# A two-layer gMLP and dilated-attention trunk in fp32: where the terms of a seven-product matrix multiplication are formed, on which engine, and when the first stage's side loads are issued

## Chip, cores and metric

The kernel runs on one core of a Trainium2 chip. TensorE (PE) multiplies 128x128 weight tiles with blocks of up to 512 columns and sums in PSUM banks; VectorE (DVE), ScalarE (ACT) and GpSimd (POOL) work on tiles of 128 partitions; SyncE (SP) and ACT issue the DMAs that bring data in and out. Each engine works through its own queue in order and waits on semaphores of the others. The metric is the device time of one launch in microseconds (us).

## What is computed

The input x is 1024 positions by 1024 channels, in float32. Two layers follow each other, each with a token mixer and a squared-ReLU MLP, all with RMS norms ahead and residual sums behind. The MLP and the skeleton, with the MLP width 4096:

```python
def reference(x, mix_norm_g, mlp_norm_g, final_norm_g, a_w_in, a_ln_g, a_ln_b, a_w_s, a_b_s,
              a_w_out, b_w_qkv, b_w_out, rel_bias, w_up, w_down):
    h = x
    for layer in range(DEPTH):
        y = _rms_norm(h, mix_norm_g[layer])
        j = layer // N_MIXERS
        if layer % N_MIXERS == 0:
            y = _chunk_gating_mixer(y, a_w_in[j], a_ln_g[j], a_ln_b[j], a_w_s[j], a_b_s[j], a_w_out[j])
        else:
            y = _dilated_attention_mixer(y, b_w_qkv[j], b_w_out[j], rel_bias)
        h = h + y
        y = _rms_norm(h, mlp_norm_g[layer])
        h = h + jnp.square(jax.nn.relu(y @ w_up[layer])) @ w_down[layer]
    return _rms_norm(h, final_norm_g)
```

The gating mixer of layer 0 makes u and v (1024 columns each) by a GELU of a matrix product, normalizes v, mixes it over the 128 positions of a chunk with a causal 128x128 matrix for each of 8 channel groups (`a_w_s`, with the bias `a_b_s`), multiplies by u, and projects. The attention of layer 1 has three groups of 8 heads of width 64 with windows and dilations (128, 1), (512, 4), (2048, 16), and 4608 columns of q, k and v.

## The kernel before

**Tiles.** The residual h lies in SBUF as eight blocks `h[k]` of 128 channels by 1024 positions; most work is done in halves of 512 positions, s = 0 and 1. A float32 matrix is used as a high part (`hi`, rounded to the matmul format, written by ACT at L203 or with a scale at L517) and a low part (`lo`, the remainder, written by VectorE at L204 or L518); a product is three matmuls, hi.hi, lo.hi, hi.lo (L180). So each operand tile costs one ACT and one VectorE instruction ahead of TensorE. Weights arrive by SP's queue in a ring of four buffers `r` (L169).

**The start.** `w_v`, the half of the first weights that makes v, is used in three passes `gi` over chunks of 128 positions (three, three and two); in each pass k runs over the eight channel blocks, with 18 matmuls per k in the first two passes. In pass 0 `load_x(0, k)` (L508) brings the block of the first half, and `scaled(0, k)` makes its two parts, the tiles called y (L517, L518), and the squares for the norm (L252 on ACT, L261 on GpSimd). From k = 4 on, pass 0 also loads two blocks of the second half for each k; in pass 1 `scaled(1, k)` makes their parts, right where TensorE uses them. `gate_weights`, added at k = 1 of pass 0, loads the causal matrices and their bias on ACT's queue (L532, L537), masks them on GpSimd (L533), splits them (`wsh`, `wsl`, L203) and forms `rb` from a matmul with ones. `spatial`, added at the start of pass 1, normalizes v chunk by chunk and does the chunk mixing with `wsh`, `wsl` and `rb`.

**Seven products.** The wide products (MLP up, q/k/v) use a scheme with seven products of half blocks in place of eight. `Terms` holds the seven x operands: t[1], t[2], t[3] are plain blocks of the normalized input (`keep` for the first half of the positions, `raws` for the second), and t[4] to t[7] are differences of them: with y0, y1 the two channel halves of `keep` and z0, z1 those of `raws`, they are z0 - y0, z1 - t1, z1 - z0 and (z1 - z0) - t2 in the code's names. `first` and `second` are generators that make the blocks and differences (L469 the block, L476 and L477 two differences on VectorE, L478 and L479 two on GpSimd); `rest` splits two of the four terms of each block later (with a copy on GpSimd, L490). This is done three times: for the MLP of layer 0, for the attention and for the MLP of layer 1. While the terms aren't ready, the first two pairs of output tiles are made the plain way (`classical`), four PSUM banks for each half; in `mlp` these are evicted by `squared` (Relu at L688, Square at L689), in the attention by `out` (L1079 for v tiles, L1121 on ACT and L1122 on VectorE for the two parts of q and k). Then `mlp` goes on with the products for q = 2: the first product's bank is copied by `first_sum` (L750) so that it can be used again.

**Order.** TensorE's order is that of the code, with a `Flow`: generators added by `flow.add` yield a modelled time or an event, and `flow.pump()`, called between groups of matmuls, lets those go on whose time has come by the model. ACT, VectorE, GpSimd and SP are ordered by a scheduler; `tc.high_priority(offset=PRIO)` moves an instruction ahead there. In the attention, `attention()` is such a generator: the scores of a unit are matmuls of k and q (at L180, with 64 partitions).

## Time and profile before

| | us |
|---|---|
| median of 3 runs | 2182.33 |
| lowest, highest | 2180.11, 2182.43 |
| the profiled execution | 2182.13 |
| its span in the trace | 2180.4 |

The profile is of one execution. Its span begins with the first and ends with the last instruction; the other 1.7 us lie around it. TensorE is busy in nearly all of it. In a timeline row stand the start, the length, engine, line, operation, the names of the tiles written and read, the shape and the count of merged instructions; in brackets the idle time ahead and what ended it. A row of windows has the busy time and count of each engine in a stretch, the clock that TensorE was granted as a share of full speed, and the share of the DMA engines' time.

### The profile page before, as it was taken

How to read it: one execution, taken by the hardware profiler on the slowest of the kernel's cores; microseconds unless marked ns; L12 is line 12 of the kernel's file. 1: busy time of each engine (PE TensorE's matmuls, PEld its weight loads, DVE VectorE, ACT ScalarE, POOL GpSimd, SP SyncE). 2: the span in 40 equal slices, each digit the busy share in tenths (PEclk: the TensorE clock that was granted, in tenths of full speed). 3: DMA queues.
4: the chain of work that ended last, by engine and by line, in shares of the span. 5: the costliest groups of instructions: out<-in, count | busy, mean ns of one | idle time of the engine just before them, and what ended most of it. 6: DMA issues, size and time to landing. Idle time of an engine off the chain costs nothing.

```text
span 2180.4 us, 30158 instructions
## 1 busy us (share of the span) xinstructions
PE 2121.8 (97%) x10242; PEld 1755.2 (80%) x10242; DVE 1647.1 (76%) x2987; ACT 1126.3 (52%) x2266; POOL 600.9 (28%) x442
## 2 busy tenths in 40 slices
PE   7999999999999999998999999999999999999998
PEld 5888887888878888886888788887878888788887
DVE  5875349676689888878787877878786666988886
ACT  5743225555564444346665656665455555544443
POOL 1100115333223322533212222201343232333345
PEclk9999999999999999999999999999999999999999
DMA  6221213456354444321211111141055543644432
GB/s 222 87 88 45 62 41 96 158 189 198 138 176 160 159 141 137 105 82 39 52 46 46 43 48 45 46 147 62 20 169 193 184 159 113 203 150 146 157 104 78
DMA packets 158814, 247.04 MB, mean 113 GB/s; under 512 B 33481, under 2 KB 47940, under 8 KB 158660
## 3 DMA queue, kind: packets, MB, share of 16 engines
q1 hardware_dynamic: 157760, 243.89, 34.3%
q8 instruction: 80, 1.31, 0.2%
q10 hardware_dynamic: 900, 1.23, 0.2%
q14 instruction: 74, 0.61, 0.1%
HBM read 180.41 MB, written 64.66 MB: 112 GB/s over the span
## 4 chain that ended last, share of the span: by engine, by line
PE 82%; DVE 9%; ACT 3%; issue 2%; DMA 2%; POOL 0%; SPq 0%; DVEq 0%; ACTq 0%; POOLq 0%
PE at L180 41%; PE mm L180 39%; PE at L187 2%; DVE wp L204 2%; DVE t L204 1%; ACT t L1219 1%; ACT wp L203 1%; DVE k L1122 1%; DMA t<-hid 1%; DVE tr L204 0%; DMA r<-in_w_v 0%; DVE h L332 0%; DVE q L1122 0%; DVE h L893 0%; DMA h<-hd 0%
## 5 line engine op out<-in xcount | busy, mean ns | idle before, releaser
L203 ACT ACTIVATE wp<-r 128x512 fp32r<-128x512 f32 (+3 forms) x492 | 295.1, 605 | 458.0 <-PE at L180 287.7
L180 PE MATMUL mm<-y,wp 128*128 128x512 f32 x1608 | 405.2, 398 | 12.8 <-ACT t L750 6.6
L180 PE MATMUL at<-hx,wp 128*128 128x512 f32 x1770 | 413.8, 390 | 3.8 <-DVE wp L204 2.2
L204 DVE TENSOR_TENSOR wp<-r,wp 128x512 fp32r<-128x512 f32 (+3 forms) x492 | 380.9, 778 | 40.1 <-ACT wp L203 36.3
L180 PEld LDWEIGHTS at<-hx,wp 128*128 128x128 f32 x1770 | 331.8, 188 | 75.1 <-DVE h L893 3.3
L180 PEld LDWEIGHTS mm<-y,wp 128*128 128x128 f32 x1608 | 303.2, 191 | 80.4 <-ACT t L750 7.5
L180 PE MATMUL at<-t,wp 128*128 128x512 f32 x1344 | 314.3, 389 | 0.0
L180 PEld LDWEIGHTS at<-t,wp 128*128 128x128 f32 x1344 | 252.7, 188 | 52.7 <-DVE t L756 0.2
L401 POOL TENSOR_TENSOR t<-r 128x512 f32<-128x512 f32 (+3 forms) x78 | 112.8, 1446 | 624.8 <-DMA r<-in_w_dn 270.3
L403 POOL TENSOR_TENSOR r<-r 128x512 f32<-128x512 f32 (+3 forms) x78 | 118.4, 1518 | 326.9 <-DVE wp L204 320.1
L180 PE MATMUL mm<-t,wp 128*128 128x512 f32 x768 | 192.6, 398 | 0.0
L204 DVE TENSOR_TENSOR hx<-t,hx 128x512 fp32r<-128x512 f32 x192 | 179.8, 948 | 5.7 <-ACT hx L203 5.6
L261 POOL TENSOR_TENSOR t<-t 128x512 f32<-128x512 f32 (+1 forms) x54 | 69.1, 1280 | 387.3 <-ACT t L252 385.4
L180 PE MATMUL mm<-hx,wp 128*128 128x512 f32 x708 | 171.8, 389 | 0.0
L180 PEld LDWEIGHTS mm<-t,wp 128*128 128x128 f32 x768 | 141.2, 189 | 29.8
L180 PE MATMUL mm<-y,whi 128*128 128x512 f32 x512 | 158.1, 390 | 0.0
L180 PEld LDWEIGHTS mm<-hx,wp 128*128 128x128 f32 x708 | 132.8, 188 | 28.1 <-DVE b L919 0.6
L893 DVE TENSOR_TENSOR h<-h,at 128x512 f32<-128x512 f32 x144 | 97.5, 679 | 55.4 <-PE at L180 55.3
L180 PE MATMUL at<-y,wp 128*128 128x512 f32 x552 | 138.1, 391 | 0.0
L756 DVE TENSOR_TENSOR t<-t,at 128x512 f32<-128x512 f32 x116 | 79.0, 683 | 74.9 <-PE at L180 74.7
L203 ACT ACTIVATE hx<-t 128x512 fp32r<-128x512 f32 x192 | 118.4, 628 | 27.8 <-DMA t<-hid 23.4
L406 POOL TENSOR_TENSOR r<-r 128x512 f32<-128x512 f32 (+3 forms) x78 | 107.2, 1374 | 79.8 <-issue 54.0
(213 smaller groups left out, 3244.0 us busy)
## 6 DMA issues: line engine op xcount, KB each, us to landing
t<-hid SPq DMA_DIRECT2D x194, 256.0 KB, 5.0
hid<-t SPq DMA_DIRECT2D x140, 256.0 KB, 2.7
r<-in_w_up SPq DMA_DIRECT2D x128, 256.0 KB, 2.8
r<-in_w_dn SPq DMA_DIRECT2D x88, 256.0 KB, 2.7
r<-in_w_qkv SPq DMA_DIRECT2D x72, 256.0 KB, 2.6
hid<-b SPq DMA_DIRECT2D x56, 256.0 KB, 2.7
r<-in_w_v SPq DMA_DIRECT2D x48, 256.0 KB, 3.0
h<-in_xT SPq DMA_DIRECT2D x16, 256.0 KB, 4.5
```

The source lines that it names most:

```text
L180: nc.tensor.matmul(out, lhsT, rhs, **kw)
L187: nc.tensor.transpose(out, src, ident)
L203: nc.scalar.activation(hi, src, AF.Copy)
L204: nc.vector.tensor_tensor(lo, src, hi.bitcast(F32), op=ALU.subtract)
L261: nc.gpsimd.tensor_tensor(self.acc, self.acc, sq, op=ALU.add)
L401: tt(r3, r[0, 0], r[1, 0], op=ALU.subtract)
L403: tt(r[1, 1], r[1, 0], r[0, 0], op=ALU.subtract)
L406: tt(r[0, 0], r[0, 1], r[1, 1], op=ALU.subtract)
L756: nc.vector.tensor_tensor(out, x, y, op=ALU.add)
L893: engine.tensor_tensor(hs[i, s], hs[i, s], src, op=ALU.add)
L1122: nc.vector.scalar_tensor_tensor(lo, a, sc, hi.bitcast(F32), op0=ALU.mult, op1=ALU.subtract)
L1219: nc.scalar.activation(p[:, c], p[:, c], AF.Exp, bias=m, scale=-1.0, accum_out=dn)
```

## The change

- The gate's weights: `gate_weights` is added at k = 7 of pass 0 and issues its four loads and two masks first, then the splits; `rb` is formed with high priority, and an event `rb_done` is set behind it, which `spatial` waits for. The loads of the second half of x begin at k = 6 of pass 0, one for each k, and go on in pass 1; `scaled(1, k)` is called one k earlier.
- The terms: `second` forms all four differences of a block on VectorE, in place (only the one that is t[6] needs a further tile), and splits t[6] and t[7]; `rest` splits t[5] and t[4], after the flow has been moved on until `second` is done (`formed`). GpSimd has no part in it.
- The MLP's first pairs: the four Relus are issued first with high priority, the four Squares behind them without.
- The spill of h to memory (`hd`) ahead of the attention is issued in `second` rather than after `rest`, and the four evictions of the attention's second half are written in another order.

```diff
--- before.py
+++ after.py
@@ -442,7 +442,7 @@
         def __init__(self):
             self.blocks = {(j, s): [] for j in range(2) for s in range(2)}
             self.t = {1: self.blocks[0, 0], 2: self.blocks[1, 0], 3: self.blocks[1, 1], 4: [], 5: [], 6: [], 7: []}
-            self.kept = []
+            self.kept, self.formed = [], False
 
         def first(self, sq, gi):
 
@@ -458,7 +458,7 @@
                 yield LAT["tile"]
                 self.blocks[k // 4, 0].append(x)
 
-        def second(self, sq, gi):
+        def second(self, sq, gi, then=None):
             r = sq.rms()
             yield 2 * LAT["rms"]
             pb = spread(r)
@@ -470,29 +470,36 @@
                     x = pair().split(y)
                     yield LAT["tile"]
                     self.blocks[j, 1].append(x)
-            tt = nc.vector.tensor_tensor
-            for k, two in enumerate(raws):
-                (z0, z1), (y0, y1), t1, t2 = *([t[:, j, :] for j in range(2)] for t in (two, self.kept[k])), spare(), spare()
-                tt(t1, z0, y0, op=ALU.subtract)
-                tt(t2, z1, t1, op=ALU.subtract)
-                nc.gpsimd.tensor_tensor(y0, z1, z0, op=ALU.subtract)
-                nc.gpsimd.tensor_tensor(y1, y1, t2, op=ALU.subtract)
-                yield 2 * LAT["tile"]
-                self.t[5].append(pair("t1").split(t1))
-                self.t[6].append(pair("t2").split(t2))
+            if then:
+                then()
+            tt, sums = nc.vector.tensor_tensor, []
+            for k in range(5):
+                if k < 4:
+                    z, y, t = raws[k], self.kept[k], temp()
+                    tt(y[:, 0, :], z[:, 0, :], y[:, 0, :], op=ALU.subtract)
+                    tt(t, z[:, 1, :], y[:, 0, :], op=ALU.subtract)
+                    tt(y[:, 1, :], y[:, 1, :], t, op=ALU.subtract)
+                    sums.append(t)
+                if k:
+                    self.t[6].append(pair("t6").split(sums[k - 1]))
+                yield LAT["tile"]
+            for k in range(5):
+                if k < 4:
+                    tt(raws[k][:, 0, :], raws[k][:, 1, :], raws[k][:, 0, :], op=ALU.subtract)
+                if k:
+                    self.t[7].append(pair("t7").split(raws[k - 1][:, 0, :]))
+                yield LAT["tile"]
+            self.formed = True
 
         def rest(self):
 
-            for k, x in enumerate(self.kept):
-                t3, t4 = x[:, 0, :], x[:, 1, :]
-                if k == 3:
-                    t4 = temp()
-                    nc.gpsimd.tensor_copy(t4, x[:, 1, :])
-                self.t[7].append(pair("t3").split(t3))
-                self.t[4].append(pair("t4").split(t4))
-
-    def start_terms(sq, s, gi, terms):
-        flow.add((terms.second if s else terms.first)(sq, gi), (1 + s) * LAT["sum"])
+            flow.until(lambda: self.formed)
+            for i, p in ((0, 5), (1, 4)):
+                for x in self.kept:
+                    self.t[p].append(pair(f"t{p}").split(x[:, i, :]))
+
+    def start_terms(sq, s, gi, terms, *then):
+        flow.add((terms.second if s else terms.first)(sq, gi, *then), (1 + s) * LAT["sum"])
 
 
     vg = {}
@@ -526,23 +533,30 @@
 
     def gate_weights():
 
+        parts = []
         for i in range(2):
             wsr = temp()
             w3 = wsr.rearrange("p (g t) -> p g t", g=4)
             nc.scalar.dma_start(w3, w_s[:, 4 * i:4 * i + 4, :])
+            bs = temp()
+            nc.scalar.dma_start(bs, b_s[:, i * HALF:(i + 1) * HALF].partition_broadcast(P))
             nc.gpsimd.affine_select(w3, w3, pattern=[[0, 4], [1, P]], compare_op=ALU.is_ge, fill=0.0,
                                     base=0, channel_multiplier=-1)
-            split(wsh[:, 4 * i:4 * i + 4, :], wsl[:, 4 * i:4 * i + 4, :], w3)
-            bs = temp()
-            nc.scalar.dma_start(bs, b_s[:, i * HALF:(i + 1) * HALF].partition_broadcast(P))
-            yield 6000
+            parts.append((wsr, bs))
+        yield 5000
+        for i, (wsr, bs) in enumerate(parts):
+            split(wsh[:, 4 * i:4 * i + 4, :], wsl[:, 4 * i:4 * i + 4, :], wsr.rearrange("p (g t) -> p g t", g=4))
             ps = at_bank()
             matmul(ps, ones, wsr, passes=4, start=True, stop=True)
-            for g in range(4):
-                m = 4 * i + g
-                nc.vector.scalar_tensor_tensor(rb[:, m, :], ps[:, blk(g)], vec[:, 6, m:m + 1],
-                                               bs[:, blk(g)], op0=ALU.mult, op1=ALU.add)
-
+            with tc.high_priority(offset=PRIO):
+                for g in range(4):
+                    m = 4 * i + g
+                    nc.vector.scalar_tensor_tensor(rb[:, m, :], ps[:, blk(g)], vec[:, 6, m:m + 1],
+                                                   bs[:, blk(g)], op0=ALU.mult, op1=ALU.add)
+            yield 2000
+        rb_done.t = flow.t
+
+    rb_done = Event()
     v_done = [Event() for _ in range(8)]
     gated = [Event() for _ in range(8)]
 
@@ -564,6 +578,7 @@
                 split(hi, lo, t)
                 parts.append((hi, lo))
             yield LAT["gate"]
+            yield rb_done, 0
             for i in range(2):
                 hi, lo = parts[i]
                 ps = at_bank()
@@ -593,19 +608,21 @@
         for k in range(KT):
             if gi == 0:
                 load_x(0, k)
-                if k >= 4:
-                    load_x(1, 2 * k - 8)
-                    load_x(1, 2 * k - 7)
             if gi == 0:
                 scaled(0, k)
             w = weight(w_v[k])
-            if gi == 0:
-                if k == 1:
-                    flow.add(gate_weights())
+            if gi == 0 and k > 5:
+                load_x(1, k - 6)
+            if gi == 0 and k == 7:
+                scaled(1, 0)
+                flow.add(gate_weights())
             if gi == 1:
+                if k < 6:
+                    load_x(1, k + 2)
                 if k == 0:
                     flow.add(spatial())
-                scaled(1, k)
+                if k < 7:
+                    scaled(1, k + 1)
             if k == 0:
                 for i, n in enumerate(chunks):
                     for f in range(2):
@@ -730,7 +747,9 @@
             for b, (q, i) in zip(banks, tiles):
                 c[q, i, s] = temp()
                 with tc.high_priority(offset=PRIO):
-                    squared(c[q, i, s], b)
+                    nc.scalar.activation(c[q, i, s], b, AF.Relu)
+            for q, i in tiles:
+                nc.scalar.activation(c[q, i, s], c[q, i, s], AF.Square)
                 what = {(0, 0): 1, (1, 0): 2, (0, 1): (0, 1), (1, 1): 3}[i, s]
                 kept(q, {what: c[q, i, s]})
             if s == 0:
@@ -995,12 +1014,18 @@
     xa = Terms()
     firsts = []
 
+    hd = [dram.tile([P, S], F32, tag=f"hd{k}", name=f"hd{k}", bufs=1) for k in range(KT)]
+
+    def spill():
+        for k in range(KT):
+            nc.sync.dma_start(hd[k], h[k])
+
     def begin_attention(sq):
         if not firsts:
             firsts.extend(plain(qkv(*t)) for t in (((0, 0), (0, 1)), ((0, 2), (1, 0))))
             start_terms(sq, 0, 2, xa)
         else:
-            start_terms(sq, 1, 2, xa)
+            start_terms(sq, 1, 2, xa, spill)
 
     mlp(0, terms, first, [(half(s), begin_attention) for s in range(2)])
 
@@ -1479,16 +1504,14 @@
         classical(xa, firsts, s, banks)
         if s == 1:
             U[0].bias = bias_tile(U[0].hp, U[0].g)
-        for b, tile in zip(banks, ((0, 0), (0, 1), (0, 2), (1, 0))):
+        outs_ = list(zip(banks, ((0, 0), (0, 1), (0, 2), (1, 0))))
+        for b, tile in outs_[2:] + outs_[:2] if s else outs_:
             out(tile, s, b)
         if s == 0:
             w = Weights(qkv(*quads[0]), late=FIRST)
             for _ in w.steps():
                 pass
     xa.rest()
-    hd = [dram.tile([P, S], F32, tag=f"hd{k}", name=f"hd{k}", bufs=1) for k in range(KT)]
-    for k in range(KT):
-        nc.sync.dma_start(hd[k], h[k])
 
     for n, two in enumerate(quads):
         wn = Weights(qkv(*quads[n + 1])) if n + 1 < len(quads) else None
```

In the compiled programs' order, three places.

ACT's queue at the start, in pass 0 of the first stage. `whi<-r` is the high part of a weight tile, `wsh<-t` that of the spatial matrices, `y<-h_94` that of x block 2 and `y<-h_95` that of block 3 (h_92 is block 0). Before:

```order
L203 ACTIVATE whi<-r 128x512 x3
L203 ACTIVATE wsh<-t 128x512
L203 ACTIVATE whi<-r 128x512 x3
L517 ACTIVATE y<-h_94,vec 128x512
L252 ACTIVATE t<-h_94 128x512
L532 DMA t<-in_w_s 128x512
L537 DMA t<-in_b_s 128x512
L203 ACTIVATE whi<-r 128x512 x2
L203 ACTIVATE wsh<-t 128x512
L203 ACTIVATE whi<-r 128x512 x2
L517 ACTIVATE y<-h_95,vec 128x512
L252 ACTIVATE t<-h_95 128x512
```

and now:

```order
L203 ACTIVATE whi<-r 128x512 x3
L524 ACTIVATE y<-h_94,vec 128x512
L252 ACTIVATE t<-h_94 128x512
L203 ACTIVATE whi<-r 128x512 x2
L524 ACTIVATE y<-h_95,vec 128x512
L252 ACTIVATE t<-h_95 128x512
L203 ACTIVATE whi<-r 128x512 x3
L524 ACTIVATE y<-h_96,vec 128x512
L252 ACTIVATE t<-h_96 128x512
L203 ACTIVATE whi<-r 128x512 x2
L524 ACTIVATE y<-h_97,vec 128x512
```

The spatial matrices' loads and splits no longer stand between the y rows; their loads stand behind the y of block 7 and of block 0 of the second half, further down. SP's queue, which is not shown, now has x block 2 as the 9th of its loads where it was the 14th, and block 3 as the 13th where it was the 22nd; the second block in such a row of two before was the second half's.

ACT's queue in the MLP of layer 0 behind the first pairs of the second half, where L688 and L689 (now L750 and L752) are Relu and Square of the four banks and L750 (now L769) is the `first_sum`. The same rows stand in the MLP of layer 1. Before:

```order
L203 ACTIVATE wp<-r 128x512
L688 ACTIVATE t<-at 128x512
L203 ACTIVATE wp<-t 128x512
L203 ACTIVATE wp<-r 128x512
L688 ACTIVATE t<-at 128x512
L689 ACTIVATE t<-t 128x512
L688 ACTIVATE t<-mm 128x512
L689 ACTIVATE t<-t 128x512
L688 ACTIVATE t<-mm 128x512
L689 ACTIVATE t<-t 128x512 x2
L750 ACTIVATE t<-mm 128x512
L203 ACTIVATE t_3249<-t 128x512
```

and now:

```order
L203 ACTIVATE t_3245<-keep 128x512
L203 ACTIVATE wp<-r 128x512
L750 ACTIVATE t<-at 128x512
L203 ACTIVATE wp<-t 128x512
L203 ACTIVATE wp<-r 128x512
L750 ACTIVATE t<-at 128x512
L750 ACTIVATE t<-mm 128x512 x2
L752 ACTIVATE t<-t 128x512 x3
L769 ACTIVATE t<-mm 128x512
L752 ACTIVATE t<-t 128x512
L203 ACTIVATE t_3248<-keep 128x512
L203 ACTIVATE t_3251<-keep 128x512
```

The `first_sum` moved ahead of the last Square; seven splits of `keep` stood ahead of the first of these rows, where now there are five.

TensorE's queue at the attention's start, behind the last plain products of the second half; `at<-k,q` are the scores of the first unit, `mm<-y,wp` of 6 matmuls the last plain ones and further ones the first products, `at<-ident,t` transposes of the softmaxed scores. Before:

```order
L180 MATMUL mm<-y,wp 128x512 x6
L180 MATMUL at<-y,wp 128x512 x6
L180 MATMUL mm<-y,wp 128x512 x27
L180 MATMUL at<-k_8534,q_8530 128x128 x2
L180 MATMUL at<-k_8535,q_8530 128x128 x2
L180 MATMUL at<-k_8534,q_8531 128x128 x2
L180 MATMUL at<-k_8534,q_8530 128x256 x2
L180 MATMUL at<-k_8535,q_8530 128x256 x2
L180 MATMUL at<-k_8534,q_8531 128x256 x2
L180 MATMUL mm<-y,wp 128x512 x3
```

and now:

```order
L180 MATMUL mm<-y,wp 128x512 x6
L180 MATMUL at<-y,wp 128x512 x6
L180 MATMUL mm<-y,wp 128x512 x9
L180 MATMUL at<-k_8536,q_8532 128x128 x2
L180 MATMUL at<-k_8537,q_8532 128x128 x2
L180 MATMUL at<-k_8536,q_8533 128x128 x2
L180 MATMUL at<-k_8536,q_8532 128x256 x2
L180 MATMUL at<-k_8537,q_8532 128x256 x2
L180 MATMUL at<-k_8536,q_8533 128x256 x2
L180 MATMUL mm<-y,wp 128x512 x12
L187 MATMUL at<-ident,t 128x128 x4
L180 MATMUL mm<-y,wp 128x512 x9
```

The scores stood behind 21 matmuls of the first products and now stand behind three. On VectorE, 33 rows (differences, splits of terms and weights) stand between the last split of a y and the low part of the k that these scores use. SP's queue has the spill of h at the same place in both programs.

## Prediction

> **What bounds the kernel now.** I read the page's head, busy times and chain first.
>
> ```profile
> span 2180.4 us, 30158 instructions
> PE 2121.8 (97%) x10242; PEld 1755.2 (80%) x10242; DVE 1647.1 (76%) x2987; ACT 1126.3 (52%) x2266; POOL 600.9 (28%) x442
> PE 82%; DVE 9%; ACT 3%; issue 2%; DMA 2%; POOL 0%; SPq 0%; DVEq 0%; ACTq 0%; POOLq 0%
> ```
>
> TensorE works for 2121.8 of 2180.4 us, and the change takes no matmul away. So it can only win in the 58.6 us in which TensorE idles, and where matmuls run at a lower granted clock. The second view is TensorE's waits by releaser (total us, times, longest):
>
> ```profile
> PE at L180 <- ACT y L517: 8.5, 3, 3.7
> PE mm L180 <- ACT t L750: 6.6, 2, 4.3
> PE at L180 <- ACT whi L203: 5.8, 1, 5.8
> PE mm L180 <- ACT t L1079: 5.6, 1, 5.6
> ```
>
> The whi wait is the unavoidable first load. The others lie where the change works: y is the scaled x of the first stage, L750 the `first_sum` of the two MLPs, L1079 an eviction of the attention's first pairs. The third view, windows (length, busy time and count of PE, PEld, DVE, ACT, POOL, then granted clock, DMA share, GB/s), shows what follows them:
>
> ```profile
> 15.85:19.26 3.41, 0.00 (x0) 0.00 (x0) 1.88 (x3) 2.46 (x5) 0.00 (x0) 1.00 0.90 321
> 19.26:22.67 3.41, 3.27 (x7) 2.29 (x8) 2.58 (x4) 1.87 (x4) 1.28 (x1) 0.50 0.85 235
> 29.50:32.91 3.41, 3.20 (x7) 2.21 (x8) 0.95 (x2) 0.47 (x1) 1.46 (x1) 0.50 0.70 208
> 370.83:374.24 3.41, 3.41 (x10) 2.63 (x9) 3.41 (x4) 1.26 (x2) 2.71 (x2) 0.50 1.05 346
> 995.47:1002.30 6.83, 4.95 (x17) 3.62 (x17) 6.83 (x10) 6.70 (x11) 2.58 (x4) 0.50 0.26 77
> 1592.80:1596.21 3.41, 3.24 (x8) 2.57 (x9) 2.74 (x3) 2.82 (x6) 2.65 (x2) 0.50 0.98 357
> ```
>
> Behind each of these stalls the clock is 0.50 for 3.41 us or twice that. At half clock 3.41 us do the work of 1.71, so each such window costs 1.71 us beside the stall.
>
> **The start.** TensorE's timeline (start, us, idle before and its releaser):
>
> ```profile
> 19.40 1.58 PE L180 MATMUL at<-whi,y 128*128 128x512 f32 x2 [3.68 <-ACT y L517]
> 29.50 0.79 PE L180 MATMUL at<-whi,y 128*128 128x512 f32 x1 [3.13 <-ACT y L517]
> 30.50 0.79 PE L180 MATMUL at<-whi,y 128*128 128x512 f32 x1 [0.21 <-DVE y L518]
> 57.03 0.50 PE L180 MATMUL at<-whi,y 128*128 128x512 f32 x1 [1.70 <-ACT y L517]
> 58.08 0.50 PE L180 MATMUL at<-whi,y 128*128 128x512 f32 x1 [0.55 <-DVE rv L233]
> ```
>
> Why the y's are late stands in the rows of ACT, POOL and SP's queue, and in the DMA issues (count, KB, median us to landing):
>
> ```profile
> 18.62 0.72 ACT L517 ACTIVATE y<-h,vec 128x512 fp32r<-128x512 f32 x1
> 25.53 0.64 POOL L533 TENSOR_SCALAR_AFFINE_SELECT t<-t 128x512 f32<-128x512 f32 x1 [4.24 <-DMA t<-in_w_s]
> 26.20 0.63 ACT L203 ACTIVATE wsh<-t 128x512 fp32r<-128x512 f32 x1 [4.68 <-POOL t L533]
> 28.73 0.72 ACT L517 ACTIVATE y<-h,vec 128x512 fp32r<-128x512 f32 x1 [0.86 <-DMA h<-in_xT]
> 56.22 0.75 ACT L517 ACTIVATE y<-h,vec 128x512 fp32r<-128x512 f32 x1
> 11.25 1.53 SPq L169 DMA_DIRECT2D r<-in_w_v  x3
> t<-in_w_s ACTq DMA_DIRECT2D x2, 256.0 KB, 6.8
> h<-in_xT SPq DMA_DIRECT2D x16, 256.0 KB, 4.5
> ```
>
> The y at 18.62 had five more rows of ACT ahead of it than it has now, four weight splits and one of the spatial weights. For the y at 28.73, ACT first stood 4.68 us at the split of the spatial weights (they come late over the same DMA engines), then 0.86 us for its x block. Both go: those splits now stand behind the last y of the pass, and x block 2 is the 9th of SP's loads instead of the 14th, block 3 the 13th instead of the 22nd. TensorE uses a block for 18 matmuls, 4.24 us by the 18 in the row 987.47 below. With blocks 0 and 1 it was done at 19.40 - 3.68 = 15.72, so it wants block 3 at 15.72 + 4.24 = 20.0 if block 2 is there in time. Block 3 now stands right behind the eighth weight load, which is the first of the row 11.25; with the 4.5 us of its own row it lands near 16.2. Block 2 stands four loads further ahead. I take the two stalls as gone. The y at 56.22, behind three evictions of VectorE's statistics stage in ACT's queue, is now computed one step sooner. Gone are 3.68 + 3.13 + 0.21 + 1.70 + 0.55 = 9.27 us and the two half-clock windows at 19.26 and 29.50, 3.41 together: 12.7.
>
> What is late next: `spatial` now also waits for `rb_done`. Queued behind that wait is TensorE's first gate work; its loads stand behind the last y of the pass, which is made about one block ahead of TensorE's use (5.8 + 1.7 for the first half clock + 7 x 4.24 = 37), so near 33 to 37; by the 6.8 us row they land by 44, and the first gate matmuls stand near 57. Their splits share ACT with the evictions of the pass. The price is between nothing and the 6.8 us landing plus two masks of 0.64, 8.1; I take 1.5, near the waits of 1.70 and 0.55 that stood here. **Start: 12.7 - 1.5 = 11.2 us saved (4.6 to 12.7).**
>
> **The two MLPs.** ACT and TensorE around the first sum; the fifth row is the second MLP's, and the last is the window in which the first one's differences are formed:
>
> ```profile
> 358.63 0.63 ACT L203 ACTIVATE t<-b 128x512 fp32r<-128x512 f32 x1 [2.02 <-DVE b L477]
> 367.62 1.16 ACT L689 ACTIVATE t<-t 128x512 f32<-128x512 f32 x2
> 368.65 0.61 ACT L750 ACTIVATE t<-mm 128x512 f32<-128x512 f32 x1
> 369.31 4.22 PE L180 MATMUL mm<-y,wp 128*128 128x512 f32 x12 [2.35 <-ACT t L750]
> 1592.31 0.61 ACT L750 ACTIVATE t<-mm 128x512 f32<-128x512 f32 x1
> 340.74:360.83 20.09, 20.09 (x88) 15.85 (x87) 19.64 (x19) 7.33 (x14) 14.17 (x9) 1.00 0.11 28
> ```
>
> The sum frees TensorE's next bank. Ahead of it in ACT's queue stood seven splits of kept blocks, four Relus and four Squares. Two things move it forward. Only five of those splits and three Squares now stand ahead: 3 rows less at 0.52 us (half of 1.16 less the overlap), 1.6 us. And ACT, which stood 2.02 us for VectorE's difference, gets the differences sooner: the last row above shows 19 VectorE rows in 19.64 us, where a row that GpSimd leaves alone takes 0.6 (row 985.22 below); that is 8.2 us of slowing. VectorE takes on 8 of GpSimd's differences per use, 8 x 0.6 = 4.8, and so is 3.4 us sooner. Together 5.0: the sum ended at 368.65 + 0.61 = 369.26 and will end near 364.3; TensorE wants it at 369.31 - 2.35 = 366.96. The stall goes, and with it the half-clock window at 370.83: 2.35 + 1.71 = **4.06 us (0 to 4.06)**. Three Squares now end behind the sum; nothing but their copies to memory waits for them.
>
> The second MLP has the same order of rows. Its sum ended at 1592.92 and will end near 1587.9; TensorE wants it 4.3 us before 1592.97, at 1588.7. So 4.28 + 1.71 = **5.99 us (0 to 5.99)**, with 0.8 us to spare.
>
> **The attention's start.** GpSimd no longer takes half of the differences.
>
> ```profile
> 985.22 1.28 DVE L204 TENSOR_TENSOR t<-b,t 128x512 fp32r<-128x512 f32 x2
> 992.64 3.41 DVE L204 TENSOR_TENSOR t<-b,t 128x512 fp32r<-128x512 f32 x2
> 992.04 1.78 POOL L478 TENSOR_TENSOR keep<-raws 128x512 f32<-128x512 f32 x1 [1.29 <-DVE b L476]
> 996.25 1.05 ACT L1079 ACTIVATE t<-mm 128x512 f32<-128x512 f32 x1
> 987.47 4.24 PE L180 MATMUL mm<-y,wp 128*128 128x512 f32 x18
> 997.35 4.21 PE L180 MATMUL mm<-y,wp 128*128 128x512 f32 x9 [5.65 <-ACT t L1079]
> 1000.11 1.07 DVE L1122 SCALAR_TENSOR_TENSOR k<-at,k 128x512 fp32r<-128x512 f32 x1
> 971.70:997.30 25.60, 20.01 (x91) 16.24 (x89) 22.04 (x22) 11.28 (x20) 15.85 (x10) 0.96 0.06 22
> ```
>
> Two splits took VectorE 1.28 us alone and 3.41 us beside GpSimd's differences at 992.04 and after: 1.1 us more a row. In the last window 22 rows take 22 us, against 13.2 at 0.6.
>
> But the scores move. Before, TensorE ran 6 + 21 matmuls ahead of them; now 6 + 3, which end near 989.5. The scores wait for q and k, whose last split stands behind 33 VectorE rows from 971.7 on. At 0.6 us that is 19.8, plus 1.1 for each of three rows that still lie beside GpSimd's weight sums: 994.8, where it was 1001.1 by the row 1000.11. TensorE so idles some 5.5 us where it idled 5.65, and the half-clock stretch stays: **0.5 us saved**. The ends: 6 us lost, if half of the 33 rows keep the window's 1.0 us (17 x 0.4 = 6.6 later), and 4 us won, if the eviction of the fourth bank, which set the stall of before, no longer limits it and VectorE's waits shrink as in the MLPs (3.4).
>
> A rule bears on the change itself. The Trainium skill, page "Perfetto Trace Analysis", section "Optimizing Scalar/DVE Operations", says: with a saturated VectorE, giving work to ScalarE or GpSimd may make sense, but GpSimd and VectorE share an SBUF read port, so moving work between those two might not help. The first half speaks against this change, the second for it; the rows 985.22 and 992.64 agree with the second, and the first is a rival below.
>
> The clock terms rest on the windows. The Trainium skill, page "TensorE: Matmul & The Clock Gate", Part 1, grants half rate after at least one idle window of about 3.4 us. By that rule the 2.35 us stall at 369.31 would cost no slow window and the sum would be 1.7 us smaller; the row 370.83 shows one at 0.50, so the measurement decides.
>
> **Moves that cost nothing.** The spill of h is written elsewhere in the code, but SP's queue has it in the same place. The attention's other eviction order leaves ACT's rows as they were. The fused gate weights issue the same four DMAs, later.
>
> **Sum.** 11.2 + 4.06 + 0.5 + 5.99 = 21.75, of which I hold 0.5 back for the second MLP's narrow margin: 21.2. The profiled run took 2182.13 us (span 2180.4 and 1.7 around it), 0.2 below the median of 2182.33. 2182.1 - 21.2 = **2161 us**. With every term at its better end the saving is 12.7 + 4.06 + 4 + 5.99 = 26.8, 2155; at the worse end 4.6 - 6 = -1.4, 2183.5.
>
> **Rivals.**
> A. Loads become the start's new wait: weights are loaded through a ring of four buffers, and the DMA share was already 0.90 in the window 15.85. One of the two stalls (3.13 + 0.21 + 1.71) then stays: 2161 + 5 = 2166. Against it: by the row 11.25 the eighth weight load was issued then, 1.4 us for each, where TensorE needs one each 2.1. Chance 0.18.
> B. The attention's stall goes as well, if q and k are split 5 us sooner than I work out: 2156. Chance 0.10.
> C. Slower: in attention the 33 VectorE rows ahead of k run at the 1.7 us of row 992.64, not 0.6: 33 x 1.1 = 36 us, all on TensorE's wait, 2161 + 36 = 2197. It turns into a loss from 21.2 / 1.1 = 19 slow rows. For it: 22 rows took 22 us. Against: only GpSimd's four weight sums remain there. Chance 0.05.
> D. The change doesn't do what it says: the Squares or the late weights hold the same banks, each stall is replaced by one of its size: 2182. Chance 0.06.
> E. VectorE's 4.8 us more per use are the limit, with no slow rows won back: both MLP stalls stay and attention loses 4.8: 2182.1 - 11.2 + 4.8 = 2176. That is what the first half of the Trainium skill's rule in "Optimizing Scalar/DVE Operations" would make of it. Chance 0.06.
>
> **Numbers.** My forecast has 0.55. The range 2154 to 2174 takes in A and B, the better ends, and at its upper side the forecast without both MLP terms (2161 + 10 = 2171) or with the attention's loss (2161 + 6.5); it leaves out C, D and E, 0.17. Faster by over 0.2% (4.4 us, about what a measurement of this kernel tells from no change): forecast, A, B, E, 0.89; same: D, 0.06; slower: C, 0.05.
>
> **What would show it.** Right: no wait for y of 3 us before 40 us and clock 1.00 there; no wait on the `first_sum` in either MLP; VectorE's differences at 0.6 us; the scores of the first unit after a wait of 5 to 6 us for k. Wrong: waits for whi or h before 40 us; a wait for rb or wsl near 57 of over 2 us; a stall over 8 us at the scores.

## The result and the profile after

The changed kernel takes 2174.04 us (median of 5 runs, 2172.50 to 2176.04), the kernel before 2182.43 (median of 5, 2180.11 to 2184.73): ratio 0.9959, 95% interval 0.9945 to 0.9974. That is 8.4 us faster, where 21.2 were forecast. The profiled run was the slowest of its five (2176.04 us, span 2174.3), so its trace accounts for 6.1 us.

The page's busy times, and TensorE's waits by releaser (total us, times, longest). Here and below, the rows of a fence are picked out and need not follow each other directly.

```profile
PE 2125.6 (98%) x10242; PEld 1761.5 (81%) x10242; DVE 1638.4 (75%) x3011; ACT 1124.9 (52%) x2264; POOL 560.6 (26%) x415
```

```profile
PE at L180 <- DVE y L525: 5.3, 1, 5.3
PE at L180 <- ACT k L1146: 5.2, 1, 5.2
PE at L187 <- ACT t L1244: 4.4, 6, 2.5
...
PE at L180 <- ACT rsb L531: 1.7, 1, 1.7
PE at L180 <- ACT vg L603: 1.7, 2, 0.8
...
PE at L180 <- DVE rv L233: 1.5, 1, 1.5
```

The late y's of the first pass and both waits on the `first_sum` (L769 now) are gone; the 5.3 us for y are the wait for the first loads, which was 5.8 us for whi before. New are a wait for k, and a group of small waits of the first stage: for rv and rsb (steps of the norm factors) and for vg (the evicted v). TensorE runs the same 10242 matmuls in both kernels, and their order differs only in the first 400 or so and at the attention's start; so the start of the n-th matmul in the two traces shows where time was won and lost:

| n-th matmul | place | before, us | after, us | lead, us |
|---|---|---|---|---|
| 145 | first stage, just after pass 0 | 50.94 | 39.95 | 11.0 |
| 400 | after the second pass change | 101.87 | 96.82 | 5.0 |
| 1300 | ahead of the first MLP's plain pairs | 291.43 | 286.42 | 5.0 |
| 1680 | behind its `first_sum` | 382.27 | 372.89 | 9.4 |
| 4300 | ahead of the attention's first products | 978.17 | 969.13 | 9.0 |
| 4547 | behind its first units' scores | 1036.89 | 1032.95 | 3.9 |
| 7600 | ahead of the second `first_sum` | 1578.78 | 1577.73 | 1.0 |
| 7700 | behind it | 1607.52 | 1600.66 | 6.9 |

The two MLPs brought 4.4 and 5.8 us (forecast 4.06 and 5.99). Pass 0 brought 11.0, of which 6.0 were given back at the pass changes. The attention's start lost 5.1. From matmul 4547 to 7600 the order is the same in both kernels, and yet another 2.9 us are lost: this trace has 23.9 us of windows at half clock there, the profile of before 13.7. In a second trace of the changed kernel (e11 below) there are 6.8, and 3.7 us are won. So this term is scatter between executions and not the change.

TensorE's waits at the first and at the second pass change, the two rows of ACT ahead of the first of them, a window before it and one behind:

```profile
44.09 0.72 PE L180 MATMUL at<-whi,y 128*128 128x512 f32 x2 [1.46 <-DVE rv L233]
45.89 1.22 PE L180 MATMUL at<-whi,y 128*128 128x512 f32 x2 [0.84 <-ACT vg L603]
53.31 1.10 PE L180 MATMUL at<-t,ones 128*128 128x512 f32 x2 [1.73 <-ACT rsb L531]
```

```profile
89.27 1.05 PE L180 MATMUL at<-ones,t 128*128 128x1 f32 x8 [0.82 <-ACT vg L603]
```

```profile
41.06 1.20 ACT L203 ACTIVATE whi<-r 128x512 fp32r<-128x512 f32 x2 [4.10 <-DMA r<-in_w_v]
42.28 1.28 ACT L231 ACT_TABLE_LOAD   x1
```

```profile
35.00:40.00 5.00, 5.00 (x28) 4.26 (x27) 2.93 (x4) 1.96 (x4) 1.19 (x2) 1.00 1.00 350
45.35:48.76 3.41, 2.87 (x5) 1.72 (x6) 2.89 (x7) 3.41 (x7) 0.00 (x0) 0.50 0.00 1
```

TensorE reaches the end of pass 0 at 38 us. ACT then stands 4.10 us at the split of a weight tile of pass 1 whose load is late; the table load for the square root is behind that split in its queue, so the bank with the sums of squares (rv) and the banks with v (vg) come free late. The DMA engines are full from 35 to 40 us (share 1.00, 350 GB/s). A half-clock window follows.

At the second pass change ACT stands 3.96 us for a weight tile as well, where it stood 2.04 in the kernel before, and its evictions to vg come behind. Its row, SP's row for that load, and a window ahead:

```profile
86.03 1.20 ACT L203 ACTIVATE whi<-r 128x512 fp32r<-128x512 f32 x2 [3.96 <-DMA r<-in_w_v]
83.32 0.96 SPq L169 DMA_DIRECT2D r<-in_w_v  x2
80.00:85.00 5.00, 5.00 (x24) 4.15 (x23) 5.00 (x13) 1.27 (x2) 0.00 (x0) 1.00 0.24 65
```

Here the DMA engines are not full: their share is 0.24. SP issued this load only at 83.32 us, after it had waited 4.1 us for VectorE's split to free a buffer of the ring, and VectorE was busy for the whole 5 us.

The MLP's `first_sum` and TensorE's next product, in the first and the second MLP:

```profile
358.52 0.60 ACT L769 ACTIVATE t<-mm 128x512 f32<-128x512 f32 x1
1584.46 0.61 ACT L769 ACTIVATE t<-mm 128x512 f32<-128x512 f32 x1
```

```profile
361.79 2.88 PE L180 MATMUL mm<-y,wp 128*128 128x512 f32 x12
1587.48 2.88 PE L180 MATMUL mm<-y,wp 128*128 128x512 f32 x12
```

Both sums end over 2 us before TensorE wants the bank, and neither product has an idle time in front of it. With the lead of 5.0 and 1.0 us at these places added, the sums end at 364.1 and 1586.1 us in the time of the profile before; 364.3 and 1587.9 were forecast.

The attention's start on TensorE, with VectorE's row for k and two windows of it:

```profile
986.33 0.58 PE L180 MATMUL at<-k,q 64*128 64x256 f32 x2 [5.22 <-ACT k L1146]
987.74 0.80 PE L180 MATMUL at<-k,q 64*128 64x256 f32 x4 [0.83 <-DVE k L1147]
988.47 5.49 PE L180 MATMUL mm<-y,wp 128*128 128x512 f32 x12
999.19 0.33 PE L187 MATMUL at<-ident,t 128*128 128x128 f32 x1 [2.53 <-ACT t L1244]
```

```profile
986.57 1.12 DVE L1147 SCALAR_TENSOR_TENSOR k<-at,k 128x512 fp32r<-128x512 f32 x1
```

```profile
984.02:994.26 10.24, 7.10 (x21) 5.32 (x22) 9.47 (x14) 8.83 (x15) 2.56 (x2) 0.50 0.16 51
1001.09:1007.92 6.83, 6.83 (x25) 5.32 (x26) 2.32 (x10) 2.63 (x10) 0.00 (x0) 0.50 0.11 41
```

The wait for k is 5.22 + 0.83 = 6.05 us, close to the 5.5 worked out. But it isn't the end of it: 10.24 us at half clock from 984.02 on, another wait of 2.53 us for the softmax (the kernel before, with products left to run, waited 1.30 there) and 6.83 us more at half clock. Between matmul 4300 and 4547 the idle times add up to 11.2 us, before to 10.1; the rest of the 5.1 us lost is matmuls at half clock.

### The profile page after: what moved, and what is told of

Same layout as the page of the kernel before. It is cut to its first block, busy times and chain, and to the rows that moved or that the text cites. A ratio compares the mean times of both kernels' runs of the same rounds, so it can differ in the third digit from the quotient of the medians.

```text
span 2174.3 us, 30115 instructions
## 1 busy us (share of the span) xinstructions
PE 2125.6 (98%) x10242; PEld 1761.5 (81%) x10242; DVE 1638.4 (75%) x3011; ACT 1124.9 (52%) x2264; POOL 560.6 (26%) x415
## 4 chain that ended last, share of the span: by engine, by line
PE 84%; DVE 6%; ACT 3%; DMA 3%; issue 3%; SPq 0%; POOL 0%; DVEq 0%; ACTq 0%; POOLq 0%
PE at L180 42%; PE mm L180 40%; PE at L187 2%; DVE wp L204 1%; DMA t<-hid 1%; DMA r<-in_w_v 1%; ACT t L1244 1%; DVE k L1147 1%; DMA h<-in_xT 1%; ACT wp L203 1%; DVE h L332 0%; DVE tr L204 0%; DVE q L1147 0%; DVE h L912 0%; DMA h<-hd 0%
## 5 line engine op out<-in xcount | busy, mean ns | idle before, releaser
L204 DVE TENSOR_TENSOR wp<-r,wp 128x512 fp32r<-128x512 f32 (+3 forms) x492 | 374.7, 765 | 42.3 <-ACT wp L203 38.6
```

What stands on the lines that cost most here:

```text
L204: nc.vector.tensor_tensor(lo, src, hi.bitcast(F32), op=ALU.subtract)
```

## The experiments

All kernels were timed in five rounds beside the kernel before. The table's last five columns are worked out like the one above: the lead over the profile of before that a kernel's trace wins in a stage (MLP 1 from matmul 1300 to 1680, attention from 4300 to 4547, MLP 2 from 7600 to 7700). e1 and e3 run the attention of before, so their -2.9 and -3.1 show how far that stage differs by itself, and that the profile of before caught it at its best.

| kernel | time, us | ratio, interval | to 145 | 145-400 | MLP 1 | attention | MLP 2 |
|---|---|---|---|---|---|---|---|
| changed | 2174.04 | 0.9959 (0.9945-0.9974) | 11.0 | -6.0 | 4.4 | -5.1 | 5.8 |
| changed again (e11) | 2172.34 | 0.9944 (0.9932-0.9956) | 10.8 | -9.0 | 4.4 | -4.3 | 5.7 |
| e1 Squares alone | 2182.24 | 0.9985 (0.9975-0.9995) | -0.9 | -1.5 | 0.4 | -2.9 | 1.0 |
| e2 terms alone | 2177.40 | 0.9961 (0.9949-0.9974) | 1.1 | 0.0 | 4.4 | -4.1 | 5.7 |
| e3 start alone | 2182.57 | 0.9991 (0.9983-1.0000) | 10.7 | -9.2 | -0.3 | -3.1 | -0.1 |
| e4 scores late | 2168.98 | 0.9928 (0.9916-0.9940) | 12.3 | -10.5 | 4.4 | 1.3 | 5.7 |
| e5 e4, x delayed | 2168.39 | 0.9931 (0.9918-0.9943) | 11.2 | -9.3 | 4.3 | 1.9 | 5.8 |
| e6 e4, gate at k = 1 | 2163.16 | 0.9907 (0.9893-0.9920) | 4.2 | 2.8 | 4.4 | 1.8 | 5.7 |
| e7 e4, v evicted first | 2170.18 | 0.9935 (0.9921-0.9948) | 11.5 | -10.6 | 4.4 | 1.2 | 5.7 |
| e8 e4, half on GpSimd | 2183.84 | 0.9998 (0.9989-1.0007) | 11.6 | -6.3 | 0.1 | -6.1 | -0.6 |
| e9 e6, splits 20 us later | 2169.84 | 0.9935 (0.9922-0.9948) | 1.5 | 1.4 | 4.4 | 2.3 | 5.8 |
| e10 e6, gate at k = 4 | 2170.01 | 0.9933 (0.9921-0.9944) | -1.4 | 2.8 | 4.4 | 1.1 | 5.7 |
| e12 e4, fewer loads | 2163.09 | 0.9902 (0.9888-0.9915) | 10.4 | -5.3 | 4.4 | 2.0 | 5.6 |

**e1: the Squares alone**, on the kernel before.

```diff
                 with tc.high_priority(offset=PRIO):
-                    squared(c[q, i, s], b)
+                    nc.scalar.activation(c[q, i, s], b, AF.Relu)
+            for q, i in tiles:
+                nc.scalar.activation(c[q, i, s], c[q, i, s], AF.Square)
```

> The kernel before with one edit: in the MLPs the four Relus first, the four Squares behind them without priority. Theory 1 (the order of ACT's rows is worth 1.6 us and VectorE's faster differences 3.4, both are needed): the first sums end 1.6 to 2.1 us sooner, so stalls of some 0.5 and 2.5 us stay on the first_sum, 2178 to 2180 us, 2 to 4 us faster than before. Rival 1 (the Squares alone held the sum): both stalls go with their half-clock windows, 10 us faster, 2172. Rival 2 (the kept-block splits and VectorE hold it alone): under 1 us faster.

TensorE's rows at the two sums:

```profile
370.66 3.06 PE L180 MATMUL mm<-y,wp 128*128 128x512 f32 x12 [1.27 <-ACT t L752]
381.20 3.01 PE L180 MATMUL at<-t,wp 128*128 128x512 f32 x12 [2.05 <-DVE t L758]
```

```profile
1597.40 3.03 PE L180 MATMUL mm<-y,wp 128*128 128x512 f32 x8 [2.96 <-ACT t L752]
```

The waits shrink by 1.1 and 1.3 us, less than the 1.6 to 2.1 of theory 1, and a wait of 2.05 us behind the first is new. In the trace the two stages win 1.4 us together; timed, e1 is 3.4 us faster. Rival 1, by which the Squares alone held the sum, falls.

**e2: the terms alone**: the whole of `Terms`, `rest`, the spill and the attention's part, with the old start and `squared` as before.

```diff
+        def second(self, sq, gi, then=None):
...
+                    tt(y[:, 0, :], z[:, 0, :], y[:, 0, :], op=ALU.subtract)
+                    tt(t, z[:, 1, :], y[:, 0, :], op=ALU.subtract)
+                    tt(y[:, 1, :], y[:, 1, :], t, op=ALU.subtract)
...
+            flow.until(lambda: self.formed)
```

> The kernel before with the terms of the change (all four differences on VectorE in place, the other split order, the flow moved on in rest, the spill and the attention's eviction order), with the old start and the old Squares. Theory 1: VectorE's 3.4 us sooner remove the first MLP's stall of 2.35 with its clock window and all but about 1 us of the second's 4.28, and the attention's start loses some 5 us as in the trace of the changed kernel: about 2180, 2 to 4 us faster than before. Rival (VectorE's extra rows hold it up, the Squares did the work): the stalls on the first_sum stay, the attention's loss shows, 2187.

Neither MLP waits for its sum any more: 4.4 and 5.7 us, all that the whole change wins there. The attention's loss is there too. So the terms carry the MLPs' gain without the Squares. The expectation was too low: it left 1 us of the wait in the second MLP, where none is left, and had e2 2 to 4 us faster, where it is 8.3.

**e3: the start alone.**

> The kernel before with the start of the change alone (gate weights and the second half's loads later, rb_done). Theory (trace of the changed kernel: 11 us gained by the end of pass 0, 6 given back at the pass changes): 5 us faster, 2177, with the first_sum stalls of 2.35 and 4.28 unchanged. Rival (what was given back belongs to the disturbed clock of one run): 8 us or more faster, 2174.

The diff is that of the change in `gate_weights`, `spatial` and the loop over `gi`. 10.7 us are won by matmul 145, 9.2 given back by 400. Timed, it is 0.0 to 0.17% faster: 2 us in the middle, where the theory had 5 and the rival 8 or more.

**e4: the scores late.** The changed kernel with the modelled time put back behind `rest`, so that TensorE's scores stand behind 21 matmuls of the first products again.

```diff
-    flow.add(attention())
     for s in range(2):
...
+    now = flow.t
     xa.rest()
+    flow.t = now
+    flow.add(attention())
```

> The changed kernel, but the modelled time is put back after rest in the attention and the attention's flow is added there, so that the first unit's scores again stand behind 6 + 21 matmuls as before. Theory A (the place of the scores turned VectorE's gain into a loss: TensorE waits for k where it had 18 matmuls that were ready, and the pieces behind keep the clock at a half): the wait of 5 to 6 us for k goes or falls below 2 us, the attention's start gains 5 to 9 us against the changed kernel, 2166 to 2169. Rival B (whatever order, TensorE waits there for banks that ACT frees late, as before the change, where it waited 5.65 us for an eviction): the stall stays 4 to 6 us with another releaser, within 2 us of the changed kernel, 2172 to 2176. Rival C (the weight sums on GpSimd, slowed by VectorE's new rows, hold VectorE's queue 3 us, so the q and k splits stay at the same time): half of it, 2169 to 2171.

TensorE's rows there:

```profile
981.75 4.24 PE L180 MATMUL mm<-y,wp 128*128 128x512 f32 x18
990.63 4.21 PE L180 MATMUL mm<-y,wp 128*128 128x512 f32 x9 [4.64 <-ACT t L1104]
994.77 0.97 PE L180 MATMUL at<-k,q 64*128 64x128 f32 x12
```

The wait for k is gone, and a wait of 4.64 us for an evicted bank stands in its place, as rival B said; yet the stage is 6.4 us shorter than in the changed kernel, as theory A said. The difference lies behind the wait: the half-clock windows between 960 and 1045 us last 13.7 us in sum, in the changed kernel 20.5, and the waits for the softmax fall from 4.4 us in sum to 0.7, since there are products left to run. In time it is 0.9928 against 0.9959 and 0.9944.

**e8: half of the differences back on GpSimd**, on e4, all else the same.

```diff
-                    tt(y[:, 1, :], y[:, 1, :], t, op=ALU.subtract)
+                    nc.gpsimd.tensor_tensor(y[:, 1, :], y[:, 1, :], t, op=ALU.subtract)
...
-                    tt(raws[k][:, 0, :], raws[k][:, 1, :], raws[k][:, 0, :], op=ALU.subtract)
+                    nc.gpsimd.tensor_tensor(raws[k][:, 0, :], raws[k][:, 1, :], raws[k][:, 0, :], op=ALU.subtract)
```

> On e4: half of the differences (the fourth of keep and the one of raws) go back to GpSimd, in place, all orders else as in e4. Theory (VectorE's rows are slowed 1.1 us each beside GpSimd, so that VectorE alone is 3.4 us sooner): the first sums end about 3.4 us later, within 1 us of when TensorE wants them, and the attention's stall grows by 3 to 4 us: 3 to 6 us slower than e4. Rival E (VectorE's load was the limit): faster than e4 by up to 4.8 us a use. Rival (neither is on the path): within 1 us.

TensorE's waits at the three uses, and two waits of ACT ahead of the first two:

```profile
364.04 3.37 PE L180 MATMUL mm<-y,wp 128*128 128x512 f32 x9 [2.32 <-ACT t L769]
997.20 3.35 PE L180 MATMUL mm<-y,wp 128*128 128x512 f32 x7 [10.45 <-ACT t L1104]
1593.52 3.91 PE L180 MATMUL mm<-y,wp 128*128 128x512 f32 x9 [4.22 <-ACT t L769]
```

```profile
351.84 1.16 ACT L203 ACTIVATE wp<-r 128x512 fp32r<-128x512 f32 x2 [6.49 <-POOL r L406]
985.15 1.16 ACT L203 ACTIVATE wp<-r 128x512 fp32r<-128x512 f32 x2 [10.59 <-POOL r L406]
```

All that e4 won is gone: 0.9998. The first sums are waited for 2.32 and 4.22 us, as before the change (2.35 and 4.28), although the Squares are out of their way, and the attention's wait grows from 4.64 to 10.45. VectorE is the faster place for these rows although it is the busier engine; rival E falls. The loss of 15 us is far more than the 3 to 6 expected, and the slower VectorE rows are only one part of it. They do show: from 330 to 355 us VectorE is busy for 24.90 us with 25 rows, 1.0 each; in the changed kernel, at the same place in the matmuls within 0.3 us, it does 37 rows in 24.07, 0.65 each. The other part is GpSimd's queue: the sums of weights that ACT has to split stand behind the differences there, and ACT stands 6.49 and 10.59 us for them, in e4 3.4 and 5.8. The run doesn't separate the two. The Trainium skill's "Perfetto Trace Analysis", section "Optimizing Scalar/DVE Operations", doubts that work moved between GpSimd and VectorE helps, for the SBUF read port that they share; this run agrees for the move to GpSimd, with 15 us, but no run here shows the port itself.

**e7: the eviction of v first**, on e4.

```diff
-        with tc.high_priority(offset=PRIO):
+        with tc.high_priority(offset=2000 if (i, s, b) == (0, 1, None) else PRIO):
             if u.g < 2:
```

> On e4: the v tile's eviction in the attention's second half (the releaser of TensorE's 4.64 us stall there) gets a higher priority and moves ahead of k's eviction and one weight split in ACT's queue, nothing else moves. Theory (the bank that this eviction frees is all that TensorE waits for): the stall falls by the two rows, 1.1 to 1.5 us, to some 3.2, the scores wait no longer than before; 1 to 3 us faster than e4 with the clock. Rival (behind it TensorE waits for k anyway): the stall moves to k, no gain.

```profile
989.92 3.65 PE L180 MATMUL mm<-y,wp 128*128 128x512 f32 x9 [3.11 <-ACT t L1104]
1001.58 0.71 PE L187 MATMUL at<-ident,t 128*128 128x128 f32 x3 [0.64 <-ACT t L1244]
```

TensorE's row shows the wait shorter by 1.5 us, as the theory had it, but the stage isn't (1.2 against 1.3) nor is the time. A wait of 0.64 us for the softmax and one of 0.23 for a bank are new, and the half clock lasts 13.7 us in sum as in e4, with more of it behind the wait (10.24 us from 1009.83 on, 6.83 in e4). The rival isn't it either: the wait for k is 0.7 us in both. Kernels with this order of the scores differ by 1.2 us in that stage, so a gain of less can't be seen here.

**e5: x delayed**, on e4.

```diff
+                    nc.gpsimd.tensor_copy(h[k + 2][0:1, HALF:HALF + 1], w[0][0:1, 0:1].bitcast(F32))
                     load_x(1, k + 2)
```

> On the kernel e4 (the changed one with the scores late): the loads of x blocks 2 to 7 of the second half wait for the first weights of pass 1 (a copy of one element on GpSimd ahead of each load) and so no longer stand among the weight loads near 27 to 32 us. Theory L (these loads fill the DMA engines, the first weights of pass 1 come late, ACT stands at their split some 4 us and its square root and the first evictions come late): the stall at the pass change (3.61 and 0.84 us in e4) falls below 1.5 in sum and its half-clock window goes, 3 to 5 us gained by the end of the first stage against e4. Rival A (ACT's own work at the pass change, two table loads and six evictions, sets it): the stall stays within 1 us. Rival G (the gate's loads are what crowds them): as A here.

```profile
40.14 0.63 ACT L203 ACTIVATE whi<-r 128x512 fp32r<-128x512 f32 x1 [4.38 <-DMA r<-in_w_v]
42.61 0.63 ACT L203 ACTIVATE whi<-r 128x512 fp32r<-128x512 f32 x1 [1.83 <-DMA r<-in_w_v]
```

```profile
SPq L515 <- POOL h L621: 7.9, 3, 5.7
```

ACT's last split ahead of the table load ends no sooner (at 43.24 us, in e4 at 43.10), and TensorE's waits for rv and vg at the first pass change go only from 4.45 us to 2.79. But this doesn't test theory L. SP's queue, whose waits the last fence shows (25 to 42 us), stood 5.7 us at the first of the delayed x loads for GpSimd's copy, and the weight load behind it was issued at 37.07 us, in e4 at 37.22. The delay held the weights up as well; whether these x loads alone made them late stays open.

**e6, e9, e10: the gate's place**, on e4: at k = 1 (e6), at k = 4 (e10), and at k = 1 with the splits 20 us later (e9).

```diff
-            if gi == 0 and k == 7:
-                scaled(1, 0)
+            if gi == 0 and k == 1:
                 flow.add(gate_weights())
+            if gi == 0 and k == 7:
+                scaled(1, 0)
```

> On e4: gate_weights is added at k = 1 as before the change, the second half's loads stay late. Theory G (the four gate loads near 31 to 34 us are what makes the weights of pass 1 late, and the late splits hold rsb): the stall at the pass change falls below 1.5 us, but a stall near 16 to 30 us comes back; if the late gate won the 11 us of the first pass, 8 to 10 of them are lost by matmul 145. Theory L (the second half's x loads took the DMA time in pass 0): at matmul 145 no more than 5 us are lost.

> On e6 (scores late, gate added at k = 1): the gate's four loads stay early, but its splits and rb are put 20 us later in the flow's time, into k = 6. Theory D (what the late gate costs at the pass change is its loads, which share the DMA engines with the weights of pass 1): as e6 at the pass change, no stall above 1.5 us there; the stall of 4.12 us at 24.81 in e6 shrinks if ACT's and VectorE's split rows caused it, stays if the loads did. Theory S (what it costs is ACT's and VectorE's rows for the splits and rb): the pass change stalls again by 2 us or more. At matmul 145 between e6 (4.2 us ahead of before) and e4 (12.3).

> On e6: gate_weights added at k = 4 of pass 0. If the end of the first stage is set by the stream of loads and by ACT, and TensorE's early lead is only waiting time at the pass change, then with the gate anywhere in pass 0 matmul 400 comes at the same time as in e6, 6 to 8 us ahead of before, and the total is within 2 us of e6, 2161 to 2165. If the place of the stall matters (half-clock windows twice in e6), up to 3 us faster.

TensorE's longest wait of the first stage in e6, in e9 and in e10:

```profile
24.81 1.58 PE L180 MATMUL at<-whi,y 128*128 128x512 f32 x2 [4.12 <-ACT y L524]
```

```profile
44.82 1.58 PE L180 MATMUL at<-whi,y 128*128 128x512 f32 x2 [5.25 <-ACT y L524]
```

```profile
42.82 1.58 PE L180 MATMUL at<-whi,y 128*128 128x512 f32 x2 [8.86 <-ACT y L524]
```

Wherever the gate is added, TensorE has long waits: one for a y at 25, 45 and 43 us, or, with the gate at k = 7, those at the pass changes. e6 did as theory G has it: 8.1 us less lead than e4 at matmul 145, and no wait at the first pass change. e9 has none there either, as theory D has it, but at matmul 145 its lead is 1.5 us and not between 4.2 and 12.3. Its wait at 45 us comes some 30 us behind the gate's loads, which ACT issues from 8.19 to 11.69 us, and follows the splits at 31.51. TensorE comes to the pass change 8 to 11 us later in e6 and e9 than in e4, so these runs don't tell what the loads cost there from what the splits cost. By matmul 400 the leads are 7.0, 2.9 and 1.4 us, with k = 7 between 0.9 and 5.3 in seven traces. e10's expectation (as e6) missed; e6 has the best place of those tried and is 0.9907, faster than before and than the change. With the gate earlier than k = 7 nothing is lost at the second pass change; with k = 7 2.6 to 6.3 us go there, between matmul 200 and 400, in all eight traces (e12's among them).

**e12: fewer loads**, on e4. x's second half and the gate's matrices are filled with constants; this part of the computation is replaced.

```diff
+        if s:
+            nc.gpsimd.memset(h[k][:, half(1)], 0.5)
+            return
...
-            nc.scalar.dma_start(w3, w_s[:, 4 * i:4 * i + 4, :])
+            nc.gpsimd.memset(wsr, 0.05)
...
-            nc.scalar.dma_start(bs, b_s[:, i * HALF:(i + 1) * HALF].partition_broadcast(P))
+            nc.gpsimd.memset(bs, 1.0)
```

> On e4: the loads of x's second half and the four gate loads are left out, and GpSimd fills these tiles with constants (this part of the computation is replaced); ACT's, VectorE's and TensorE's rows keep their order. 3 of the 9 MB or so that are loaded in the first 45 us are gone. Theory D (the stream of loads sets the first stage's end: TensorE's lead of 11 to 12 us at matmul 145 is given back because the weights of pass 1 come late behind the other loads): the stalls at the pass change (4.45 us in e4) fall below 1 us, no half-clock window near 45 us, matmul 400 is 7 to 10 us ahead of before instead of 1.8, the total 2160 to 2164. Rival R (the ring of four buffers and ACT's own work at the pass change set it, whatever else is loaded): the stalls stay within 1.5 us of e4's, matmul 400 not over 4 us ahead, the total within 3 us of e4's 2169.

ACT's row where it stood 4.10 us for a load, and TensorE's waits up to 100 us behind the first load:

```profile
37.34 1.18 ACT L203 ACTIVATE whi<-r 128x512 fp32r<-128x512 f32 x2 [2.40 <-PE mm L180]
```

```profile
49.58 1.10 PE L180 MATMUL at<-t,ones 128*128 128x512 f32 x2 [1.59 <-ACT rsb L534]
87.12 1.87 PE L180 MATMUL at<-ones,t 128*128 128x1 f32 x8 [2.42 <-ACT vg L606]
```

The split now waits for TensorE and not for its load, the waits for rv and vg at the first pass change are gone, no half-clock window follows, and at matmul 200 the lead is 11.4 us where e4 had 6.8. So at the first pass change it is the stream of loads, as theory D says; the run takes out both kinds together (11.70 MB up to 45 us become 8.98), and which of them weighs more isn't shown. The second pass change still takes 6.3 us, so theory D's 7 to 10 us at matmul 400 missed (5.1), though the total, 2163.09 us, lies in its range.

**e11: the changed kernel once more.**

> The changed kernel as it is, again, to see how far its stages differ between chips and runs: matmul 145 10 to 12 us ahead of the profile of before, matmul 400 2 to 5 us, the attention's segment (matmul 4300 to 4547) 4 to 6 us lost; total 0.994 to 0.997 of before.

As expected, but for matmul 400: 1.8 us ahead, a little below the 2 to 5. So between executions the first stage differs by 3 us and the attention's half-clock windows by some us: one trace's stage sums are good to about that.

## Why the prediction was wrong

**The two MLPs: right.** 4.4 us of 4.06 and 5.8 of 5.99, and both sums end over 2 us before they are wanted. Of the split into 1.6 us by the order and 3.4 by VectorE the second holds: with the terms alone (e2) everything is won, with the order alone (e1) 1.4 of 10, and with GpSimd's half back (e8) nothing, the order notwithstanding. The terms' part was sized a little low: against the moment at which TensorE wants the bank, the sums come 4.4 and 5.6 us sooner in e2, where 3.4 and 1.0 for two splits less were counted.

**The price of VectorE's rows: right.** 8 more rows and no neighbour on GpSimd made it sooner at all three uses; e8 is the test, with GpSimd's longer queue as a second cause beside VectorE's slower rows. In the attention the sum came out partly by luck. It counted three rows slowed by 1.1 us each beside GpSimd's weight sums; they weren't slowed, but VectorE stood 3.21 us at a weight split for one of these sums, which is nearly the same.

**The start: the term that failed most.** "I take the two stalls as gone" held: 11.0 us by matmul 145, 10.8 in the repeat, where 3.68 + 3.13 + 0.21 + 3.41 = 10.4 were counted for them. What failed is the paragraph "What is late next". It priced one wait, for `rb_done`, at 1.5 us, and counted the waits at 57 us as gone. It never asked whether the loads and ACT would be ready for a TensorE that comes 11 us earlier. They weren't: 1.46 + 0.84 + 1.73 + 0.82 + 0.57 us of new waits and a half-clock window. The wait that was priced, for rb, doesn't occur. Over six traces with the changed start (changed, e11, e3, e4, e7 and e8) the lead at matmul 400 is 5.05, 1.77, 1.51, 1.79, 0.88 and 5.28 us, 2.7 in the mean; over three with the old one (before, e1, e2) 0.0, -2.4 and 1.1, -0.4 in the mean. So the start is worth some 3 us and not 11.2, below the bound of 4.6. Rival A had the right cause for the first pass change, loads that become the new wait, but at the wrong place (a y of pass 0) and with 5 us where 8 are missing.

**The attention: right wait, wrong sum.** The wait for k (6.05 us for 5.5) came as worked out, behind VectorE's queue. "The half-clock stretch stays" failed: it went from 10.2 us to 20.5, and the waits for the softmax grew from 2.6 us in sum to 4.4. Part of this is the draw of one trace: the attention of before has 10.2, 17.1 and 17.1 us of half clock in its three traces (before, e1, e3), the changed order 20.5 in all three of its own (changed, e11, e2), and the kernels with the scores late 10.2 to 17.1. The stage lost 5.1, 4.3 and 4.1 us with the changed order; before's own code gives 0, -2.9 and -3.1. So the change costs some 2.5 us there and not a gain of 0.5. With the scores late (the seven kernels e4, e5, e6, e7, e9, e10 and e12) the terms win 1.1 to 2.3. The 6 us lost stood in the text as the worse end, but for VectorE's rows, which were not the reason.

**The moves at no cost: right as far as shown.** The two kernels' SP rows for the spill are the same; the eviction order alone wasn't tried.

**The sum.** 3 + 4.4 - 2.5 + 5.7 = 10.6 us by these stages, between the 8.4 and 12.3 us that the two timings of the changed kernel gave. The two traces differ by more than that in the stretch from matmul 4547 to 7600, which no part of the change touches: 2.9 us lost in one, 3.7 won in the other. So the start, some 8 us short, and the attention, 3 us short, make up what these stages lack of the 21.2.

**Left open.** Why the second pass change takes 2.6 to 6.3 us only with the gate at k = 7 wasn't settled: the order of TensorE's spatial matmuls there differs too, and e12 shows that the loads taken out are not all of it. ACT waits there for a weight that was issued late, because its buffer in the ring came free late (3.96 us in the changed kernel, 3.71 and 1.50 in e12); why that is worse with the gate at k = 7 isn't shown.

## What to carry to other kernels

A stall that is removed early in a kernel is a lead, and a lead is worth what the next stage can take: ask for each engine and for the loads whether they are ready that much sooner, and where the next queue is. Where a move makes matmuls wait for an operand, look at what stands ready behind them: ready products behind a wait cost nothing to put in front. An engine that is busier can still be the faster place, if the other one slows it or has work in its queue that a third engine waits for; one run with the work moved back shows it. Before reading a stage's loss from one trace, look how far that stage differs between traces of the same code.
